# Attention heads two at a time, and expert weights with consecutive rows per partition, in a four-layer model on one core

## The chip, the core and the metric

The kernel runs on one core of a Trainium2 chip. The metric is the device time of one execution in microseconds (us). Three runs of the kernel before gave 1328.03 to 1331.99 us, median 1330.16.

Names in the profile: PE is TensorE (matmuls), PEld its weight loads, DVE is VectorE, ACT ScalarE, POOL GpSimd, SP the engine whose queue issues most DMAs. In a matmul, "64*128" is the part of the 128x128 array that it uses: rows (the contracted dimension) times columns. `out<-in` are the program's tile names.

## The reference

One sequence of 256 tokens (and 256 context tokens) of width 1024 goes through two blocks of two layers, all in f32. Cut to what matters here:

```
# block 1, two layers, latents and context: 8 query heads of 64, 2 key/value heads
p   = rms_norm(x) * (1 + scale) + shift  @ w_in
y_b = softmax(rope(q) k^T / 8) v            # 256 context + 256 latent keys
y_a = gmlp(...); y_c = bidirectional mLSTM(...)
x   = x + gate * concat(y_a, y_b, y_c) @ w_out
# block 2, layer 0: dilated attention, 3 groups of 16 heads, band of 128 keys + own block
logits = q k^T / 8 + rel_bias ;  the three groups merged by their softmax denominators
# block 2, layer 1: forgetting attention, 16 heads, causal
logits = q k^T / 8 + cum_t - cum_s ;  p = softmax(masked logits)
# after each of the two: mixture of 16 experts, the best group of 4, the best 2 in it
hid = silu(t @ w_gate[e]) * (t @ w_up[e])   # 1024 -> 256
y   = sum_e gate[e] * hid @ w_down[e]       # 256 -> 1024
x   = x + g_f * y
```

## The kernel before, in words

The 256 latents are two tiles of 128 tokens, the context another two (T is the tile). Most products are exact to f32 by splitting each factor into two f16 parts: `mm3` issues hi*hi, hi*lo and lo*hi, `mm3p` (L271) does the same for several products, one kind after the other in turns. Splitting costs an ACT copy and a VectorE subtraction per tile of weights (`wl<-raw,wh`, L418). All matmuls have the line of the helper `mm` (L258), transposes that of `tr` (L262), so tile names tell them apart.

The work around attention is woven: every head is a generator that yields an estimate of how long its next step should wait. `lane` keeps two of them active; `tick` and `step`, called between projection matmuls, advance the one whose time has come. After that a scheduler fixes, engine by engine, the order of instructions; from then on each engine runs its queue in order. PSUM has eight banks: two for projections (`ps_mm`), two for scores (`ps_s`), two for transposes (`ps_tr`), one for attention outputs (`ps_o`), one more (`ps_ad`).

- `attention` (block 1): `head(h)` issues three score matmuls with 64 contracted rows (512 or 256 keys) into one score bank, VectorE's maximum (L980) and ACT's exponential; after a yield the transposes of the probabilities, after another the products with the values.
- `attn2` (block 2, dilated and forgetting): the same with two query tiles per head, 128 and 256 keys. VectorE adds the bias and takes the extreme in one instruction (L1530). In the forgetting attention a matmul with all 128 rows (`ps_s<-nc,s`) first writes the bias into the bank.
- `head(h)` of even h lies in rows 0 to 63 of the array, that of odd h in rows 64 to 127.

The expert stages: `x_T` transposes the tokens for the router, `gather0` and `gather` pick the tokens of each expert by a product with one-hot matrices (`ps_s<-OH,nhl`, the token tile is the stationary operand), up to 64 tokens per expert. Experts go in eight pairs P: `gate_up(P)` (moving operand: the f32 weights), transposes of the hidden values (`ps_tr<-consts,mh`), `down` and `scatter` (`oh,OHT`). `moe_gu` issues the DMAs of gate and up weights from SP, 512 KB each for even P into the `raw` tiles, 256 KB each for odd P into tiles named `x`, two pairs ahead; `moe_dn` those of the down weights (`big`, `qk`). At P = 4 a branch on overflow stands in the program; all engines meet there, and the DMAs for P = 6 are issued behind it. In DRAM a row of w_gate or w_up is 256 f32 (1 KB), one of w_down 1024 f32 (4 KB).

Of the kernel before, what the change touches and what calls it, by code (L numbers as in the profile page):

```python
# [10 lines left out]
F32 = mybir.dt.float32  # L11
# [4 lines left out]
OP = mybir.AluOpType  # L16
# [46 lines left out]
def late_arrays(a):  # L63
# [11 lines left out]
    for l in range(2):  # L75
        c[f"rb_{l}"] = rep(np.concatenate([a["router_group_b_2"][l], a["router_expert_b_2"][l]]))
        wr = np.zeros((D, 32), np.float32)
        wr[:, :20] = np.concatenate([a["router_group_w_2"][l], a["router_expert_w_2"][l]], 1)
        c[f"wr_{l}"] = wr.reshape(8, 128, 32).transpose(1, 0, 2).reshape(128, 256)
# [29 lines left out]

def rep(v):  # L110
    return np.broadcast_to(np.asarray(v).reshape(1, -1), (128, v.size))
# [6 lines left out]
def param_arrays(a):  # L118
# [6 lines left out]
    for l in range(2):  # L125
        p[f"bada1_{l}"] = feat(a["b_ada"][l])
        p[f"bada2_{l}"] = feat(a["b_ada_2"][l])
        p[f"gn_{l}"] = feat(a["g_norm"][l])
        p[f"nm_{l}"] = feat(a["norm_mix_2"][l])
        p[f"nf_{l}"] = feat(a["norm_ffn_2"][l])  # L130
# [23 lines left out]
class Stage:  # L154
# [346 lines left out]
    def ada_feat(self, blk, l, v0, gname, res):  # L501
# [3 lines left out]
        def done(p):  # L505
            sb = self.w2("adasb")
            self.act(sb, p, AF.Copy)
            q = self.ps("tr")
            for b in range(4):
                self.tr(q[:, b * 128:(b + 1) * 128], sb[:, b * 128:(b + 1) * 128])  # L510
# [140 lines left out]
    def mod_T(self, xn, mods, xT, T):  # L651
# [3 lines left out]
        for k0 in (0, 4):  # L655
            p = self.ps("tr")
            for k in range(4):
                self.tr(p[:, k * 128:(k + 1) * 128], xn[:, (k0 + k) * 128:(k0 + k + 1) * 128])
# [70 lines left out]
class Block1(Stage):  # L729
# [233 lines left out]
    def attention(self, T, q, kTh, kTl, vh, vl, ybs):  # L963
# [6 lines left out]
        def head(h):  # L970
            a, j = h % 2, h // 2
            if h == 0:
                st["den"] = self.small("den", 8)
            den = st["den"]
            r = slice(64 * a, 64 * a + 64)
            h = 4 * a + j
            s = self.ps("s")
            self.mm3(s[:, :nk], qh[r, j], ql[r, j], kTh[r, :nk], kTl[r, :nk], True, True)
            mx = self.small("mx", 1, 4)
            nc.vector.tensor_reduce(mx, s[:, :nk], axis=AX.X, op=OP.max, negate=True)  # L980
            e = self.w2("e")
            self.act(e[:, :nk], s[:, :nk], AF.Exp, bias=mx, scale=1.0, accum_out=den[:, h:h + 1])
            yield 2.8
            et = self.ps("tr")
            for b in range(nb):
                self.tr(et[:, b * 128:(b + 1) * 128], e[:, b * 128:(b + 1) * 128])
            eh = self.h1("eh")
            el = self.h1("el")
            self.hilo(eh[:, :nk], el[:, :nk], et[:, :nk])
            yield 1.8  # L990
# [3 lines left out]
            for b in range(nb):  # L994
                Tk = (b + 2) % 4
                self.mm3(o[:, h * 64:h * 64 + 64], eh[:, b * 128:(b + 1) * 128],
                         el[:, b * 128:(b + 1) * 128], vh[:, Tk, r], vl[:, Tk, r], b == 0, b == nb - 1)
            if h == 7:
# [7 lines left out]
        return [head(h) for h in range(8)]  # L1006
# [342 lines left out]
class Block2(Block1):  # L1349
# [160 lines left out]
    def attn2(self, q, k, v, bias, nm, den, U, tail, extra=None):  # L1510
# [5 lines left out]
        def head(h):  # L1516
            b4, hh = divmod(h, 4)
            j, r = h // 2, slice(64 * (h % 2), 64 * (h % 2) + 64)
            s = self.ps("s")
# [7 lines left out]
            e = self.w2("e2")  # L1527
            bt = bias(h)
            for T, (c0, c1) in enumerate(spans):
                nc.vector.tensor_tensor_reduce(e[:, c0:c1], s[:, c0:c1], bt[:, 256 - (c1 - c0):256], op0=OP.add,  # L1530
                                               op1=OP.min, scale=-1.0, scalar=1e38, accum_out=nm[:, T, h:h + 1])
            for T, (c0, c1) in enumerate(spans):
                self.act(e[:, c0:c1], e[:, c0:c1], AF.Exp, scale=-1.0, bias=nm[:, T, h:h + 1],
                         accum_out=den[:, T, h:h + 1])
            yield 2.5
            et = self.ps("tr")
            for b in range(3):
                self.tr(et[:, b * 128:(b + 1) * 128], e[:, b * 128:(b + 1) * 128])
            eh = self.h1("e2h")
            el = self.h1("e2l")  # L1540
            self.hilo(eh[:, :384], el[:, :384], et[:, :384])
            yield 1.8
            if hh == 0:
                st["o"] = self.ps("o")
            o = st["o"]
            ov = o.rearrange("p (t h d) -> p t h d", t=2, h=4)
            vs = slice(h * 64, h * 64 + 64)
            for T, kb, b, first, last in ((0, 0, 0, True, True), (1, 0, 1, True, False), (1, 1, 2, False, True)):
                bb = slice(b * 128, b * 128 + 128)
                self.mm3(ov[:, T, hh], eh[:, bb], el[:, bb], v[0][:, kb, vs], v[1][:, kb, vs], first, last)  # L1550
            if hh == 3:
                self.act(U[:, :, b4 * 4:b4 * 4 + 4, :], ov, AF.Copy)
            if h == 7:
                yield from tail()

        return [head(h) for h in range(8)]
# [310 lines left out]

    def gather0(self, T):
# [3 lines left out]
        for k in range(8):  # L1872
            for a in range(2):
                self.mm(self.g0[k // 4][:, k % 4 * 128:k % 4 * 128 + 128], self.nhl[T][a][:, k * 128:k * 128 + 128],
                        self.OH[0][:, 256 * T:256 * T + 128], T == 0 and a == 0 and k % 4 == 0, T == 1 and a == 1 and k % 4 == 3)

    def moe_gu(self, i, P, part=range(8)):
# [3 lines left out]
        for q in part:  # L1881
# [3 lines left out]
            t = self.x4(F32, (2, 512)) if P % 2 else self.raw()  # L1885
# [3 lines left out]
            ws[a].extend(t[:, j] for j in range(n))  # L1889

    def moe_dn(self, i, P):
        ws = self.W2["dn", P] = []
        for a in range(2):
            t = (self.qk(F32, (8, 256)) if P % 2 else self.big()).rearrange("p (f n) d -> p f (n d)", f=2)
            self.nc.sync.dma_start(t, self.ap["w_down"][i, 2 * P + a].rearrange("(f p) n -> p f n", p=128))
            ws.append(t)

    def moe(self, i):
# [17 lines left out]
        def gather(c, half=None):  # L1916
# [3 lines left out]
            for k2 in range(4):  # L1920
                p = self.ps("s")
                for k in (2 * k2, 2 * k2 + 1):
                    o = p[:, n * (k % 2):n * (k % 2) + n]
                    dk = slice(k * 128, k * 128 + 128)
                    for m, (T, a) in enumerate(((0, 0), (1, 0), (0, 1), (1, 1))):
                        self.mm(o, self.nhl[T][a][:, dk], OH[c][:, 256 * T + h:256 * T + h + n], m == 0, m == 3)
# [64 lines left out]
        def gate_up(P):  # L1991
# [3 lines left out]
            for k in range(8):  # L1995
                for a in range(2):
                    xs = slice((2 * (P % 2) + a) * CAP, (2 * (P % 2) + a) * CAP + CAP)
                    self.mm(p[64 * a:64 * a + 64], x[k // 4][:, k % 4, xs], wg[a][k], k == 0, k == 7,
# [27 lines left out]
        for P in range(8):  # L2026
# [15 lines left out]
            q = self.ps("tr")  # L2042
            for f in range(2):
                self.tr(q[:, f * 128:(f + 1) * 128], h[:, f * 128:(f + 1) * 128])
# [23 lines left out]
    def overflow(self, i, cnt, CAP):  # L2068
# [3 lines left out]
        with tc.If(rv > CAP):  # L2072
# [7 lines left out]
            with tc.For_i(0, 16, 1) as e:  # L2080
                raws = []
                for q in range(4):
                    t = self.wtile(("wh", "wl")[q % 2], (2, 512), F32)
                    for n, nm in enumerate(("w_gate", "w_up")):
                        nc.sync.dma_start(t[:, :, n * 256:n * 256 + 256],
                                          ap[nm][i, ds(e, 1)].rearrange("a (k p) n -> p (a k) n", p=128)[:, 2 * q:2 * q + 2, :])
# [75 lines left out]
```

## Time and profile before

| | before |
|---|---|
| three runs, median (lowest, highest) | 1330.16 (1328.03, 1331.99) us |
| profiled execution: its time, its span | 1332.35, 1330.6 us |
| mean granted TensorE clock | 0.963 |
| PE busy | 1230.0 us (92%) |
| DVE, ACT, POOL busy | 775.6 (58%), 630.6 (47%), 226.3 us (17%) |
| DMA moved | 292.36 MB in 159870 packets, mean 220 GB/s |

The stages, in us of the span: block 1 to about 545 (first layer to 320), the dilated attention 545 to 850, its expert stage 885 to 1016, the forgetting attention 1024 to 1157, its expert stage 1190 to 1323. An engine's busy share is a mean over these. A granted clock of 1.00 is 2.4 GHz for TensorE. In a timeline row the figure after the start is the length from the first start to the last end of the instructions merged in the row; an idle time in brackets is the engine's before the row, with what ended it.

### The profile page before, as it was taken

Reading aid. Unit: us, or ns where it says so; the run is one execution under the profiler, and the core shown is the slowest. Engines: PE = TensorE matmul, PEld = TensorE weight load, DVE = VectorE, ACT = ScalarE, POOL = GpSimd, SP = SyncE. Lnnn points to the kernel's source line nnn. Section 1 sums busy time; section 2 is a strip of 40 time slices with the busy share of each in tenths; the row PEclk is TensorE's granted clock in tenths of the full one; section 3 lists DMA queues with packets and bytes.
Section 4 is the critical chain, followed back from the end, with each engine's and each line's share of the span. In section 5 each row is a group of like instructions: output and inputs, shape, how many; then the busy total and the mean of one; then the engine's idle time right before and its main releaser. Section 6 shows DMA issues by size and latency. Waiting matters only on the chain. (4 is left out here: it accounts for less than half of the span.)

```text
span 1330.6 us, 21270 instructions
## 1 busy us (share of the span) xinstructions
PE 1230.0 (92%) x8064; PEld 590.9 (44%) x8064; DVE 775.6 (58%) x1787; ACT 630.6 (47%) x1373; POOL 226.3 (17%) x254
## 2 busy tenths in 40 slices
PE   6889999999999998999999999989986999989987
PEld 2434444544444444445555555445322445545332
DVE  3585646785567768756777777562114676563212
ACT  3434545553545556566767776333114556432211
POOL 1021000221330001342224222010002412010000
PEclk8899999999999999999999999889998999779989
DMA  9744455344484474687454547779998785419995
GB/s 323 258 157 159 159 174 183 123 164 144 140 271 144 167 263 156 214 300 278 166 185 132 185 164 244 253 240 328 337 325 293 287 302 187 155 46 333 331 327 192
DMA packets 159870, 292.36 MB, mean 220 GB/s; under 512 B 10890, under 2 KB 94986, under 8 KB 153876
## 3 DMA queue, kind: packets, MB, share of 16 engines
q1 hardware_dynamic: 157028, 281.57, 61.8%
q0 software_dynamic: 2736, 9.39, 2.3%
q8 instruction: 65, 1.06, 0.3%
q14 instruction: 41, 0.34, 0.1%
HBM read 288.80 MB, written 2.13 MB: 219 GB/s over the span
## 5 line engine op out<-in xcount | busy, mean ns | idle before, releaser
L258 PE MATMUL ps_mm<-wh,x 128*128 128x512 f16 (+1 forms) x1120 | 379.1, 379 | 3.6 <-DVE kn L245 1.8
L258 PEld LDWEIGHTS <-x 128*128 128x128 f16 (+1 forms) x2344 | 194.0, 98 | 250.5 <-issue 80.6
L258 PE MATMUL ps_mm<-wl,x 128*128 128x512 f16 (+1 forms) x736 | 276.8, 376 | 0.0
L418 DVE SCALAR_TENSOR_TENSOR wl<-raw,wh 128x1024 f16<-128x1024 f32 (+2 forms) x188 | 221.6, 1209 | 52.7 <-ACT wh L242 52.2
L242 ACT ACTIVATE wh<-raw 128x1024 f16<-128x1024 f32 (+2 forms) x188 | 182.2, 1015 | 47.1 <-PE ps_mm L258 40.7
L258 PE MATMUL ps_mm<-wh,y 128*128 128x512 f16 (+1 forms) x480 | 175.3, 379 | 0.0
L258 PE MATMUL ps_ad<-raw,cz 128*32 128x512 f32 (+1 forms) x640 | 113.4, 578 | 12.8 <-DMA raw<-in_w_ada 12.8
L287 POOL TENSOR_SCALAR hss<-hss 128x8 f32<-128x8 f32 (+2 forms) x58 | 18.5, 319 | 430.2 <-DVE hss L683 415.0
L288 POOL TENSOR_TENSOR hr<-hss,nhalf 128x8 f32<-128x8 f32 (+2 forms) x58 | 85.0, 1466 | 4.8
L258 PEld LDWEIGHTS <-y 128*128 128x128 f16 x560 | 55.3, 101 | 63.3 <-issue 13.0
L253 DVE SCALAR_TENSOR_TENSOR oh<-ps_tr,ka,oh 128x512 f16<-128x512 f32 x32 | 24.0, 751 | 91.5 <-ACT oh L242 88.7
L242 ACT ACTIVATE e<-e,ka 128x128 f32<-128x128 f32 (+1 forms) x128 | 56.7, 445 | 42.9 <-DVE ka L1530 41.7
L262 PE MATMUL ps_tr<-consts,e 128*128 128x128 f32 x352 | 57.7, 285 | 6.0 <-ACT e L242 3.0
L258 PE MATMUL ps_mm<-wh,big 128*128 128x512 f16 x192 | 59.5, 386 | 0.5 <-DVE big L253 0.5
L262 PEld LDWEIGHTS ps_tr<-consts,e 128*128 128x128 f32 x352 | 42.2, 144 | 28.4 <-ACT e L242 8.8
L242 ACT ACTIVATE oh<-ps_tr,ka 128x512 f16<-128x512 f32 x32 | 22.0, 687 | 58.0 <-PE ps_tr L258 58.0
L258 PE MATMUL ps_mm<-raw,wh 128*64 128x512 f32 x128 | 37.7, 665 | 8.0 <-DMA raw<-in_w_up 8.0
L245 DVE TENSOR_TENSOR el<-ps_tr,eh 128x512 f16<-128x512 f32 (+1 forms) x48 | 27.8, 597 | 29.3 <-ACT eh L242 29.0
L245 DVE TENSOR_TENSOR e2l<-ps_tr,e2h 128x384 f16<-128x384 f32 x64 | 34.8, 554 | 16.7 <-ACT e2h L242 16.4
L242 ACT ACTIVATE e2h<-ps_tr 128x384 f16<-128x384 f32 x64 | 30.4, 486 | 28.7 <-PE ps_tr L262 28.4
L242 ACT ACTIVATE e<-ps_s,mx 128x512 f32<-128x512 f32 (+1 forms) x48 | 29.3, 613 | 30.9 <-DVE mx L980 28.2
L258 PEld LDWEIGHTS ps_ad<-raw,cz 128*32 128x32 f32 x640 | 21.3, 112 | 50.5 <-issue 35.7
(377 smaller groups left out, 2005.0 us busy)
## 6 DMA issues: line engine op xcount, KB each, us to landing
raw<-in_w_ada SPq DMA_DIRECT2D x40, 1024.0 KB
raw<-in_a_w_in SPq DMA_DIRECT2D x36, 1024.0 KB
raw<-in_w_ada SPq DMA_DIRECT2D x64, 512.0 KB
raw<-in_w_in SPq DMA_DIRECT2D x16, 1024.0 KB
qk<-in_w_down SPq DMA_DIRECT2D x16, 1024.0 KB
big<-in_w_down SPq DMA_DIRECT2D x16, 1024.0 KB
x<-in_w_gate SPq DMA_DIRECT2D x64, 256.0 KB
raw<-in_w_gate SPq DMA_DIRECT2D x32, 512.0 KB
```

The costliest lines, as they stand in the source:

```text
L242: return self.nc.scalar.activation(out, in_, func, **kw)
L245: return self.nc.vector.tensor_tensor(out, a, b, op=op)
L253: return self.nc.vector.scalar_tensor_tensor(out, a, s, b, op0=op0, op1=op1)
L258: return self.nc.tensor.matmul(out, lhsT, rhs, start=start, stop=stop, **kw)
L262: return self.nc.tensor.transpose(out, in_, self.C("ident")[:n, :n])
L287: self.nc.gpsimd.tensor_scalar(in_, in_, eps, None, op0=OP.add)
L288: self.nc.gpsimd.tensor_tensor(out, in_, self.nhalf.to_broadcast(list(in_.shape)), op=OP.pow)
L418: (on or self.nc.vector).scalar_tensor_tensor(wl, raw, WS, wh, op0=OP.mult, op1=OP.subtract)
```

## The change

Two parts.

First, the order in which the 1024 features lie over partitions and tiles in the expert stages. The DMAs of w_gate and w_up give each partition four consecutive rows (4 KB in one piece for even P, and two of the four, 2 KB, for odd P) in place of single rows of 1 KB; those of w_down two consecutive rows (8 KB). So feature 4p + j of each half of 512 belongs to partition p, and all that meets the weights follows: the gather reads its stationary operand in steps of four f16 (`rows`), the transposes of the router (`x_T`), of the modulation (`nf`), and of the hidden values (`hv`) read f32 in steps of four or two, and constants are laid out anew on the host (`quad`).

Second, `head(h)` becomes `pair(j)`: both heads' score matmuls go in turns into the two score banks, then come both softmaxes, the transposes of one head (a yield of 1.0) and of the other (1.8), the values of one (0.3) and of the other. `mm3p` ties each matmul to the one before, so that the scheduler keeps them in turns. A lane now runs over four pairs in place of eight heads.

```diff
     def mm3p(self, parts, start=True, stop=True):
+        last = None
         for m in range(3):
             for o, ah, al, bh, bl in parts:
-                self.mm(o, al if m == 2 else ah, bl if m == 1 else bh, start and m == 0, stop and m == 2)
+                i = self.mm(o, al if m == 2 else ah, bl if m == 1 else bh, start and m == 0, stop and m == 2).ins
+                if last is not None:
+                    self.tc.add_manual_dep(i, last.name, mybir.DependencyInfo(
+                        mybir.DependencyClass.NoSync, mybir.DependencyReason.DATA), reason="in turns")
+                last = i
...
-            s = self.ps("s")
-            self.mm3(s[:, :nk], qh[r, j], ql[r, j], kTh[r, :nk], kTl[r, :nk], True, True)
+            s = [self.ps("s") for _ in range(2)]
+            self.mm3p([(p[:, :nk], qh[r, j], ql[r, j], kTh[r, :nk], kTl[r, :nk]) for p, r in zip(s, self.rows2)])
+            es = []
+            for a in range(2):
+                mx = self.small("mx", 1, 4)
+                nc.vector.tensor_reduce(mx, s[a][:, :nk], axis=AX.X, op=OP.max, negate=True)
...
                 if extra is not None:
-                    self.mm(s[:, c0:c1], extra[0][:, h:h + 1].to_broadcast([128, 128]), extra[1][:, :n], True, False)
+                    for p, h in zip(s, hs):
+                        self.mm(p[:, c0:c1], extra[0][:, h:h + 1].to_broadcast([128, 128]), extra[1][:, :n], True, False)
                 tq = slice(T * 128, T * 128 + 128)
-                self.mm3(s[:, c0:c1], q[0][r, j, tq], q[1][r, j, tq], k[0][r, j, :n], k[1][r, j, :n],
-                         extra is None, True)
+                self.mm3p([(p[:, c0:c1], q[0][r, j, tq], q[1][r, j, tq], k[0][r, j, :n], k[1][r, j, :n])
+                           for p, r in zip(s, self.rows2)], extra is None, True)
...
-        return [head(h) for h in range(8)]
+        return [pair(j) for j in range(4)]
...
+        xv = self.x[T][:, 512 * n:512 * n + 512].rearrange("p (n k) -> p k n", k=4)
         for k in range(4):
-            self.tr(p[:, k * 128:(k + 1) * 128], self.x[T][:, (4 * n + k) * 128:(4 * n + k + 1) * 128])
+            self.tr(p[:, k * 128:(k + 1) * 128], xv[:, k])
...
+    def rows(self, T, a, k):
+        h = self.nhl[T][a][:, k // 4 * 512:k // 4 * 512 + 512]
+        return h.rearrange("p (n j) -> p j n", j=4)[:, k % 4]
...
-                src = self.ap[nm][i, 2 * P + a].rearrange("(k p) n -> p k n", p=128)
-                self.nc.sync.dma_start(t[:, :, m * 256:m * 256 + 256], src[:, k:k + n, :])
+                src = self.ap[nm][i, 2 * P + a].rearrange("(h p j) n -> p h j n", h=2, j=4)
+                self.nc.sync.dma_start(t[:, m], src[:, k // 4, k % 4:k % 4 + n, :])
...
-            self.nc.sync.dma_start(t, self.ap["w_down"][i, 2 * P + a].rearrange("(f p) n -> p f n", p=128))
+            self.nc.sync.dma_start(t, self.ap["w_down"][i, 2 * P + a].rearrange("(p f) n -> p f n", p=128))
```

What this moves on TensorE, at two places. The first is the first pair of heads in the forgetting attention: `ps_s_11458` is the bank of one head, `ps_s_11472` (before) or `ps_s_11459` (now) that of the other, `nc3_10991` the moving operand of the bias matmul, `qk_10994` the queries and keys. Before, from the bias matmul of the first head's 256 keys on:

```order
L258 LDWEIGHTS s3_10992
L258 MATMUL ps_s_11458<-nc3_10991,s3_10992 128x256
L258 LDWEIGHTS qk_10994
L258 MATMUL ps_s_11458<-qk_10994 128x256
L258 LDWEIGHTS qk_10994
L258 MATMUL ps_s_11458<-qk_10994 128x256
L258 LDWEIGHTS qk_10994
L258 MATMUL ps_s_11458<-qk_10994 128x256
L258 LDWEIGHTS s3_10992
L258 MATMUL ps_s_11472<-nc3_10991,s3_10992 128x128
L258 LDWEIGHTS qk_10994
```

Now, from the start of the pair on:

```order
L264 LDWEIGHTS s3_10992
L264 MATMUL ps_s_11458<-nc3_10991,s3_10992 128x128
L264 LDWEIGHTS s3_10992
L264 MATMUL ps_s_11459<-nc3_10991,s3_10992 128x128
L264 LDWEIGHTS qk_10994
L264 MATMUL ps_s_11458<-qk_10994 128x128
L264 LDWEIGHTS qk_10994
L264 MATMUL ps_s_11459<-qk_10994 128x128
L264 LDWEIGHTS qk_10994
L264 MATMUL ps_s_11458<-qk_10994 128x128
L264 LDWEIGHTS qk_10994
```

Before, a bias matmul stands ahead of each run of three 64-row matmuls of one head. Now the two heads' bias matmuls stand together, and six 64-row matmuls follow them, one of each head in turns.

The second place is in the dilated attention, on TensorE again. Before, where the first head of a pair ends and the second begins (banks `ps_s_6708` and `ps_s_6720`):

```order
L258 MATMUL ps_s_6708<-qk_6266 128x256
L258 LDWEIGHTS qk_6266
L258 MATMUL ps_s_6708<-qk_6266 128x256
L258 LDWEIGHTS qk_6266
L258 MATMUL ps_s_6720<-qk_6266 128x128
L258 LDWEIGHTS qk_6266
L258 MATMUL ps_s_6720<-qk_6266 128x128
L258 LDWEIGHTS qk_6266
L258 MATMUL ps_s_6720<-qk_6266 128x128
L258 LDWEIGHTS qk_6266
```

Now, at the second of two pairs that follow each other (banks `ps_s_6804` and `ps_s_6805`; the first pair's twelve score matmuls stand 6 matmuls ahead, in turns without a break); `ps_mm` rows are projections:

```order
L264 MATMUL ps_mm_6722<-wl_6562,x2_6012 128x512
L264 LDWEIGHTS qk_6266
L264 MATMUL ps_s_6804<-qk_6266 128x128
L264 LDWEIGHTS x2_6012
L264 MATMUL ps_mm_6722<-wh_6561,x2_6012 128x512
L264 LDWEIGHTS x2_6012
L264 MATMUL ps_mm_6722<-wh_6561,x2_6012 128x512
L264 LDWEIGHTS x2_6012
L264 MATMUL ps_mm_6722<-wl_6562,x2_6012 128x512
L264 LDWEIGHTS qk_6266
L264 MATMUL ps_s_6805<-qk_6266 128x128
L264 LDWEIGHTS qk_6266
```

The second pair's first matmul stands apart from the other eleven, with three projections between. The first pair of every two is whole, in the forgetting attention too; in the order of the whole program about half of all pairs have such a break. Between two such pairs and the next two there are 73 to 171 other matmuls in the dilated attention, where before every pair stood some 51 (between units 102 to 110) from the next.

## Rows read from the trace of the kernel before

**Rows 1.** Windows by stretch (busy us and count by engine, granted clock, DMA share, GB/s).

```profile
core 0: us, PE busy (x) PEld busy (x) DVE busy (x) ACT busy (x) POOL busy (x), PEclk, DMA share, GB/s
70.00:180.00 110.00, 106.37 (x774) 48.12 (x772) 67.50 (x168) 46.67 (x104) 12.80 (x12) 0.97 0.44 145
590.00:850.00 260.00, 250.90 (x1841) 133.04 (x1840) 186.88 (x412) 174.20 (x394) 71.73 (x69) 1.00 0.60 205
885.00:1016.00 131.00, 123.93 (x630) 48.89 (x628) 34.68 (x98) 29.79 (x65) 1.17 (x2) 0.97 0.94 317
1076.00:1157.00 81.00, 80.43 (x564) 43.69 (x562) 51.99 (x123) 47.95 (x115) 13.32 (x14) 0.95 0.61 207
1190.00:1323.00 133.00, 125.05 (x624) 50.08 (x624) 34.37 (x98) 28.42 (x61) 1.16 (x2) 0.96 0.85 289
```

**Rows 2.** Timeline of TensorE around one lone head, first layer (start, us, line, operation, count).

```profile
107.75 0.38 PE L258 MATMUL ps_mm<-wl,x 128*128 128x512 f16 x1
107.96 0.38 PE L258 MATMUL ps_mm<-wh,y 128*128 128x512 f16 x1
108.27 0.82 PE L258 MATMUL ps_s<-x,x 64*128 64x512 f16 x3
109.02 0.44 PE L262 MATMUL ps_tr<-consts,qo 128*128 128x128 f32 x2
```

**Rows 3.** Timeline of TensorE, two heads next to each other, second layer.

```profile
431.78 0.83 PE L258 MATMUL ps_s<-x,x 64*128 64x512 f16 x6
```

**Rows 4.** Timeline of TensorE, two heads of the forgetting attention.

```profile
1076.66 0.22 PE L258 MATMUL ps_s<-nc,s 128*128 128x128 bf16 x1
...
1078.81 0.39 PE L258 MATMUL ps_mm<-wh,x 128*128 128x512 f16 x1
```

**Rows 5.** Timeline of TensorE, two heads of the dilated attention.

```profile
618.71 0.80 PE L258 MATMUL ps_s<-qk 64*128 64x128 f16 x12
619.43 0.39 PE L258 MATMUL ps_mm<-wh,x 128*128 128x512 f16 x1
```

**Rows 6.** Timeline of VectorE after two dilated heads.

```profile
599.52 0.29 DVE L1530 CUSTOM_DVE_ANT_0 e<-ps_s,big 128x128 f32<-128x128 f32 x1
...
599.73 0.42 DVE L1530 CUSTOM_DVE_ANT_0 e<-ps_s,big 128x256 f32<-128x256 f32 x1
...
600.08 1.22 DVE L418 SCALAR_TENSOR_TENSOR wl<-raw,wh 128x1024 f16<-128x1024 f32 x1
```

**Rows 7.** Longest wait of TensorE in each expert stage (total, times, longest).

```profile
PE ps_mm L258 <- DMA raw<-in_w_up: 3.6, 1, 3.6
...
PE ps_mm L258 <- DMA raw<-in_w_up: 4.4, 1, 4.4
```

**Rows 8.** Chain that ended last, second expert stage.

```profile
1274.03 8.61 DMA raw<-in_w_up
```

**Rows 9.** Windows: gate and up rows alone; down rows among them; after the second wait.

```profile
955.00:961.00 6.00, 6.00 (x29) 2.11 (x28) 1.49 (x2) 1.38 (x2) 0.00 (x0) 1.00 1.11 349
985.00:990.00 5.00, 5.00 (x26) 1.62 (x24) 0.21 (x1) 0.00 (x0) 0.00 (x0) 1.00 1.04 403
1280.00:1300.00 20.00, 17.23 (x61) 5.35 (x62) 1.64 (x4) 2.14 (x4) 0.00 (x0) 0.83 1.08 366
```

**Rows 10.** Timeline of TensorE before and after that wait: two scatter matmuls each.

```profile
1271.32 0.59 PE L258 MATMUL ps_o<-oh,OHT 128*128 128x512 f16 x2
...
1285.76 1.06 PE L258 MATMUL ps_o<-oh,OHT 128*128 128x512 f16 x2
```

**Rows 11.** Timeline of TensorE, a gather of 16 matmuls.

```profile
894.55 1.07 PE L258 MATMUL ps_s<-OH,nhl 128*128 128x128 f16 x16
895.45 0.55 PE L258 MATMUL ps_tr<-kb,OH 128*128 128x6 f16 x16
```

**Rows 12.** Weight loads by form (busy, mean ns, idle before).

```profile
L262 PEld LDWEIGHTS ps_tr<-consts,e 128*128 128x128 f32 x352 | 42.2, 144 | 28.4 <-ACT e L242 8.8 <-DVE qk L253 4.4 <-ACT e2h L242 0.8
...
L258 PEld LDWEIGHTS <-nhl 128*128 128x128 f16 x320 | 28.8, 108 | 12.0 <-issue 9.4
```

More of the change, by code (lines that the diff above doesn't have):

```diff
@@ L107, in feat, with quad @@
     return np.ascontiguousarray(v.reshape(-1, 128).T)
+def quad(v):
+    return np.ascontiguousarray(v.reshape(-1, 128, 4).transpose(1, 0, 2).reshape(128, -1))
 def rep(v):
@@ L968, in attention, with pair @@
         st = {}
[L970 to L972 removed]
+        def pair(j):
+            if j == 0:
                 st["den"] = self.small("den", 8)
             den = st["den"]
[L975 to L990 removed]
+            s = [self.ps("s") for _ in range(2)]
[4 more added lines that the diff above has]
+                nc.vector.tensor_reduce(mx, s[a][:, :nk], axis=AX.X, op=OP.max, negate=True)
+                e = self.w2("e")
+                self.act(e[:, :nk], s[a][:, :nk], AF.Exp, bias=mx, scale=1.0, accum_out=den[:, 4 * a + j:4 * a + j + 1])
+                es.append(e)
+            yield 2.8
+            eT = []
+            for a in range(2):
+                et = self.ps("tr")
+                for b in range(nb):
+                    self.tr(et[:, b * 128:(b + 1) * 128], es[a][:, b * 128:(b + 1) * 128])
+                eh = self.h1("eh")
+                el = self.h1("el")
+                self.hilo(eh[:, :nk], el[:, :nk], et[:, :nk])
+                eT.append((eh, el))
+                yield (1.0, 1.8)[a]
             if "o" not in st:
@@ L993, in head @@
             o = st["o"]
[L994 to L998, printed above, removed]
+            for a, r in enumerate(self.rows2):
+                h = 4 * a + j
+                eh, el = eT[a]
+                for b in range(nb):
+                    Tk = (b + 2) % 4
+                    self.mm3(o[:, h * 64:h * 64 + 64], eh[:, b * 128:(b + 1) * 128],
+                             el[:, b * 128:(b + 1) * 128], vh[:, Tk, r], vl[:, Tk, r], b == 0, b == nb - 1)
+                if not a:
+                    yield 0.3
+            if j == 3:
                 rec = self.small("rec", 8)
@@ L1514, in attn2, with pair @@
         st = {}
[L1516 to L1519, printed above, removed]
+        def pair(j):
+            hs = (2 * j, 2 * j + 1)
+            s = [self.ps("s") for _ in hs]
             for T, (c0, c1) in enumerate(spans):
@@ L1527, in head @@
[L1527 to L1534, printed above, removed]
@@ new lines, in pair @@
+            es = []
+            for p, h in zip(s, hs):
+                e = self.w2("e2")
+                bt = bias(h)
+                for T, (c0, c1) in enumerate(spans):
+                    nc.vector.tensor_tensor_reduce(e[:, c0:c1], p[:, c0:c1], bt[:, 256 - (c1 - c0):256], op0=OP.add,
+                                                   op1=OP.min, scale=-1.0, scalar=1e38, accum_out=nm[:, T, h:h + 1])
+                for T, (c0, c1) in enumerate(spans):
+                    self.act(e[:, c0:c1], e[:, c0:c1], AF.Exp, scale=-1.0, bias=nm[:, T, h:h + 1],
+                             accum_out=den[:, T, h:h + 1])
+                es.append(e)
@@ new lines, in pair @@
+            yield 2.5
+            eT = []
+            for a in range(2):
+                et = self.ps("tr")
+                for b in range(3):
+                    self.tr(et[:, b * 128:(b + 1) * 128], es[a][:, b * 128:(b + 1) * 128])
+                eh = self.h1("e2h")
+                el = self.h1("e2l")
+                self.hilo(eh[:, :384], el[:, :384], et[:, :384])
+                eT.append((eh, el))
+                yield (1.0, 1.8)[a]
+            for a, h in enumerate(hs):
+                b4, hh = divmod(h, 4)
+                if hh == 0:
+                    st["o"] = self.ps("o")
+                o = st["o"]
+                eh, el = eT[a]
+                ov = o.rearrange("p (t h d) -> p t h d", t=2, h=4)
+                vs = slice(h * 64, h * 64 + 64)
+                for T, kb, b, first, last in ((0, 0, 0, True, True), (1, 0, 1, True, False), (1, 1, 2, False, True)):
+                    bb = slice(b * 128, b * 128 + 128)
+                    self.mm3(ov[:, T, hh], eh[:, bb], el[:, bb], v[0][:, kb, vs], v[1][:, kb, vs], first, last)
+                if hh == 3:
+                    self.act(U[:, :, b4 * 4:b4 * 4 + 4, :], ov, AF.Copy)
+                if not a:
+                    yield 0.3
+                elif j == 3:
+                    yield from tail()
@@ L1558, in dilated @@
+        return [pair(j) for j in range(4)]
     def dilated(self, xT):
```

52 lines of the change are left out of this document (19 added, 33 removed).

## The prediction

> **What bounds the kernel now.** I read the windows first. In the five stretches that the change touches, TensorE is busy 106.4 of 110 us, 250.9 of 260, 123.9 of 131, 80.4 of 81 and 125.1 of 133 us [rows 1], while VectorE stays under three quarters. So time comes off where matmuls go, and is added wherever TensorE has to wait. Next I read the waits of the two expert stages: one wait each for expert weights, 3.6 and 4.4 us [rows 7], and the chain that ended last begins at the second one [rows 8]. The timeline then gives the price of the score matmuls themselves.
>
> **Scores: the prices.** A lone head with 512 keys is three matmuls over 64 rows. It starts at 108.27 and the next matmul at 109.02: 0.75 us, though three steps of 0.213 (107.75 to 107.96 is one step of ordinary 512-column matmuls, 0.21) would be 0.64; and the matmul ahead of it started 0.31 earlier instead of 0.21 [rows 2]. So each crossing between 64-row and 128-row work costs about 0.10 us. Where two heads stand next to each other, as three of one and then three of the other, six matmuls are listed with 0.83 us from the first start to the last end [rows 3], where one head's three have 0.82 [rows 2]: as long as one head alone, so 0.76 to the next start. The chip already runs both array halves together when the heads are merely adjacent; what matters is adjacency and the number of crossings, not the alternation.
>
> **Scores: the sum by stage.** (a) First layer, first two tiles (70 to 180 us): 16 heads, before nearly all alone or three matmuls apart, at 0.75 + 0.10. That is 13.6 us. Now 8 pairs at 0.76 + 0.10 = 6.9, but in the new order five of them are broken: the first head's first matmul stands alone and the other five follow some projections later (the second excerpt shows the pattern in the dilated attention). A break is two more crossings plus a lone matmul's half that no longer overlaps, 0.20 + 0.11 = 0.3; seven breaks add 2.1. Gain 13.6 - 9.0 = 4.6, taken as 4.5. (b) Forgetting attention, 8 pairs. Before, each head's bias matmul (all 128 rows) stands between the 64-row runs: 1076.66 to 1078.81 is 2.15 us a pair [rows 4], four 64-row runs with eight crossings. Serially the columns are 4 x (128 + 256) x 2 = 3072 at 0.213 us for 512, 1.28 us; the other 0.87 is eight crossings. Now there are two runs a pair: two bias matmuls of each width 0.32, the 64-row matmuls at half of 0.96 = 0.48, four crossings 0.44, sum 1.24. Gain 0.9 for the four whole pairs and 0.63 for the four broken ones: 6.1. If the halves did not overlap here, 0.48 more a pair, and the gain would be 2.3. (c) Dilated attention, 24 pairs. These already stood adjacent: twelve matmuls from 618.71 to 619.43, 0.72 us [rows 5]. Alternated they need at least 0.48 + 0.10, so a whole pair gains 0 to 0.14 (I take 0.07 for 12 of them, 0.8), while the other 12, the second of every two, are broken and lose 0.2 to 0.25 (2.7); against that, five breaks of before go (1.0). Loss about 1. Second layer of block 1 and the 256-key tiles: adjacent before, one or two more breaks now, 0.1 loss. Sum of (a) to (c): 4.5 + 6.1 - 1.1 = 9.5 us off TensorE, with 5 to 13 as bounds.
>
> **Scores: the new wait.** Two lanes now carry pairs, so one pair follows the last after some 6 to 12 projections, and both score banks must be free again. TensorE takes instructions in order, so all projections of the next lane queue behind a score matmul that waits. A dilated head leaves its bank after two VectorE instructions of 0.29 and 0.42 us (0.21 + 0.35 apart), and a weight split of 1.22 us can stand between [rows 6]. Pair 0 runs 0.65 us, six to eight fillers 1.3 to 1.7; two heads on VectorE are 1.3 us. Without a split ahead the banks are free in time; with one, TensorE waits up to 1.2 us. There are 28 such second pairs (12 in block 1, 12 dilated, 4 forgetting), so the bounds are 0 and 34 us. I take 3, one wait of 0.3 in three: VectorE has 28% slack in that stretch [rows 1], and the order puts a split between two pairs only after the first pair's reductions.
>
> **Expert weights.** The gate and up rows grow from 1 KB to 4 KB (even pairs of experts) and 2 KB (odd), the down rows from 4 to 8 KB. In a stretch where only 1 KB rows were under way the DMA gave 349 GB/s at a share of 1.11; where 4 KB rows of the down weights were among them 403 at 1.04 [rows 9]. Taking that ratio, 0.87, the transfer that TensorE waits for, 8.61 us [rows 8], shortens by 1.15 in each stage: 2.3 in all. It cannot vanish, because its issue stands behind the branch on overflow, a barrier that the change leaves. Behind the second wait two scatter matmuls take 1.06 us, and 0.59 ahead of it [rows 10]; the granted clock of the 20 us from 1280 on is 0.83 [rows 9], a part of them at the lower of its two levels, 1.2 instead of 2.4 GHz. The eight scatter matmuls pay 4 x 0.47 = 1.9 us. A shorter idle stretch may spare part; I take 1.0. Late chunks elsewhere give 0.5. Sum 3.8, bounds 0 (rows are not faster) and 15 (all idle time of both stages, 7.1 + 7.9 by [rows 1]).
> The Trainium skill's "DMA: Bandwidth & Descriptors" (Specifications) names 512 B as the size from which transfers run at line rate, and about 358 GB/s as what the HBM gives one core. By that nothing here is gained and the forecast would be 3.8 later. The 403 in [rows 9] is above that figure, so the trace does not bear it out.
>
> **Strided operands.** To match, the gather reads its stationary operand in steps of 8 bytes (320 loads), and 72 transposes read f32 in steps of 16 or 8 bytes. No row shows a strided load. From below: nothing changes, since gather matmuls of 128 columns start every 0.056 us (16 from 894.55 to 895.45 [rows 11]) while a load is listed with 98 to 108 ns [rows 12], so loads overlap. From above: the loads double and nothing hides it, 320 x 0.1 = 32 us, and 72 transposes x 2 records x 0.14 [rows 12] = 20 us more. I take 0, the nearest row being the overlap.
> By the Trainium skill's "SBUF — State Buffer" (Specifications, and the cacheline note in "SBUF: two separate sides") two accesses must fall in one 16-byte line for full speed. That clears the f16 gather and speaks against the transposes with 16-byte steps. No run here shows it. If those 40 transposes doubled, it would be up to 11 us by [rows 12].
>
> **Sum.** Own time of the profiled execution 1332.35 (span 1330.6 and 1.75 around it). 1332.35 - 9.5 + 3 - 3.8 = 1322.0. The three runs have a median of 1330.16, 2.2 below that execution: 1320.
>
> **Rivals.**
> 1. The pairs wait on their banks (slower). One mechanism: a split or another VectorE job stands ahead of the reductions of the pair before. Gains are 13.3, so the point where it turns slower by 4 is 17.3 / 28 = 0.62 us a pair, half a split. With a whole split each time: 1330 - 13 + 34 = 1351; with 0.75 us, 1338. For: the score lanes move in bursts now, four heads' exponentials and evacuations at once. Against: VectorE's slack, and almost no TensorE wait in [rows 1] for the dilated stretch. Chance 0.11.
> 2. TensorE gets shorter but stages end elsewhere. Block 1's tiles and the forgetting stage end in chains of VectorE and GpSimd; if (a) and (b) are given back there, only the expert part stays: 1330 - 3.8 + 1 = 1327. For: the first layer's two tiles leave 3.6 of 110 us idle, so not every step there waits for TensorE. Against: 80.4 of 81 us busy [rows 1]. Chance 0.18.
> 3. The expert stages are transfer-bound, and faster rows also take the clock dip and both waits: 8.0 + 2 x 1.9 = 11.8 instead of 3.8: 1312. For: DMA share 0.94 in the first stage [rows 1]. Against: TensorE is fully busy between the waits. Chance 0.15.
> 4. Strided loads cost half of their upper bound for the gather, +16: 1336. Chance 0.07.
> The forecast itself, 1313 to 1326, has 0.49.
>
> **The numbers.** A measurement of this kernel tells 0.3% (4 us) from no change. Faster: the forecast, rival 3 and a quarter of rival 2, 0.69. Same: most of rival 2, and the mild ends of 1 and 4, 0.18. Slower: the rest of rivals 1 and 4, 0.13. Range 1307 to 1336: it takes in rivals 2, 3 and 4 and leaves out most of rival 1.
>
> **What would show it.** In the forgetting stage a pair's 16 matmuls should span about 1.25 us instead of 2.15, or 1.45 broken; in the first layer six matmuls 0.76. The waits of scores on VectorE's reductions should sum to a few us; over 15 would be rival 1. The expert waits should be near 2.5 and 3.3 us, the DMA above 390 GB/s with even pairs. The gather's 16 matmuls should still take 0.90 us; above 1.5 is rival 4. I am wrong if the forgetting window does not shrink, or if the dilated stretch grows by more than 3 us.

## The result, and the profile after

The changed kernel takes 1312.0 us in the median of four executions (1307.47 to 1317.39), where the kernel before has 1331.08 beside it: ratio 0.9855, 95% interval 0.9807 to 0.9903. Two later sets, on two different chips, gave 0.9842 (0.9819 to 0.9865) and 0.9851 (0.9823 to 0.9879). The forecast was 1320 us with a range of 1307 to 1336: the right way, inside the range, and half the size. Executions of one program differ here by 4 to 18 us, mostly along with the granted clock that they get (six of the pairs-only kernel below: 1315.59 us at 0.975 to 1322.69 at 0.967), so single stages are compared over several profiles further on. The profiled execution of the changed kernel took 1307.47 us (span 1305.5, clock 0.979), its fastest.

The windows that answer to the dilated and the forgetting attention of [rows 1], moved by what had been gained until then (us, then busy us and count of PE, PEld, DVE, ACT, POOL, then granted clock, DMA share, GB/s):

```profile
591.00:844.00 253.00, 247.27 (x1827) 126.85 (x1829) 185.25 (x419) 174.24 (x398) 79.38 (x68) 1.00 0.59 202
1065.00:1137.00 72.00, 70.09 (x545) 37.52 (x543) 50.52 (x122) 46.10 (x114) 14.82 (x14) 1.00 0.68 247
```

TensorE is about as full as it was: 247 of 253 us and 70 of 72. In the forgetting attention the granted clock is 1.00 instead of 0.95. The lengths of these windows are not yet the gain, because they do not hold quite the same work (1827 matmuls of TensorE where [rows 1] had 1841, and 545 where it had 564); the stages are measured between the same instructions in the table further on.

**Score matmuls after.** First layer, TensorE's timeline: a whole pair and a broken one, answering to [rows 2, 3].

```profile
143.95 0.82 PE L264 MATMUL ps_s<-x,x 64*128 64x512 f16 x6
144.71 0.39 PE L264 MATMUL ps_mm<-wh,x 128*128 128x512 f16 x1
...
146.37 0.37 PE L264 MATMUL ps_s<-x,x 64*128 64x512 f16 x1
...
148.94 0.82 PE L264 MATMUL ps_s<-x,x 64*128 64x512 f16 x5
149.69 0.39 PE L264 MATMUL ps_mm<-wh,x 128*128 128x512 f16 x1
```

Six matmuls take 0.76 us, where a lone head's three took 0.75. In a broken pair the first matmul stands 2.6 us ahead of the other five, and those five still take 0.75.

Forgetting attention: first the 64-row matmuls of one head before, which stand inside [rows 4], then a whole pair now and the start of a broken one.

```profile
1076.81 0.34 PE L258 MATMUL ps_s<-qk 64*128 64x128 f16 x3
...
1077.30 0.50 PE L258 MATMUL ps_s<-qk 64*128 64x256 f16 x3
```

```profile
1065.49 0.28 PE L264 MATMUL ps_s<-nc,s 128*128 128x128 bf16 x2
1065.69 0.34 PE L264 MATMUL ps_s<-qk 64*128 64x128 f16 x6
1065.97 0.39 PE L264 MATMUL ps_s<-nc,s 128*128 128x256 bf16 x2
1066.29 0.50 PE L264 MATMUL ps_s<-qk 64*128 64x256 f16 x6
1066.72 0.39 PE L264 MATMUL ps_mm<-wh,x 128*128 128x512 f16 x1
...
1068.45 0.22 PE L264 MATMUL ps_s<-nc,s 128*128 128x128 bf16 x1
1068.60 0.23 PE L264 MATMUL ps_s<-qk 64*128 64x128 f16 x1
```

From 1065.49 to 1066.72 is 1.23 us; before it was 2.15, and the forecast was 1.24. Six 64-row matmuls are listed with 0.34 and 0.50 us, as long as three were.

Dilated attention, answering to [rows 5]: a whole pair, then the next one, broken, which waited 0.53 us for VectorE.

```profile
608.93 0.67 PE L264 MATMUL ps_s<-qk 64*128 64x128 f16 x12
609.53 1.07 PE L264 MATMUL ps_ad<-raw,cz 128*32 128x512 f32 x8
...
611.66 0.21 PE L264 MATMUL ps_s<-qk 64*128 64x128 f16 x1 [0.53 <-DVE ka L1556]
...
612.56 0.67 PE L264 MATMUL ps_s<-qk 64*128 64x128 f16 x11
```

A whole pair now takes 0.60 instead of 0.72 us. The waits of TensorE in the dilated stage (total us, times, longest), before from 598 to 865:

```profile
PE ps_o L258 <- DVE e2l L245: 3.7, 8, 1.3
PE ps_tr L262 <- DVE x L245: 3.2, 2, 1.7
PE ps_tr L262 <- DVE qk L253: 2.3, 9, 0.4
```

and after, from 594 to 861:

```profile
PE ps_s L264 <- DVE ka L1556: 3.8, 5, 0.8
PE ps_tr L268 <- DVE x L251: 0.9, 1, 0.9
PE ps_tr L268 <- DVE qk L259: 0.4, 2, 0.2
PE ps_o L264 <- DVE e2l L251: 0.3, 1, 0.3
```

The new wait is there with 3.8 us. What the forecast lacks is the other side: 9.2 us of waits of before became 1.6. (Before there is one wait more, 1.1 us for the weights `in_w_ada`. It is also missing with the weights alone, without pairs, so it is not counted here.)

**Expert stages after.** Their waits, first and second stage, answering to [rows 7]; the piece of the chain that answers to [rows 8]; two windows to [rows 9] and a scatter behind the second wait to [rows 10]:

```profile
PE ps_mm L264 <- DMA raw<-in_w_up: 2.0, 1, 2.0
...
PE ps_mm L264 <- DMA raw<-in_w_up: 2.2, 1, 2.2
```

```profile
1251.68 6.97 DMA raw<-in_w_up
```

```profile
964.00:970.00 6.00, 3.99 (x12) 1.54 (x11) 0.75 (x1) 1.07 (x2) 0.00 (x0) 0.74 1.02 408
970.00:976.00 6.00, 6.00 (x29) 2.00 (x29) 0.75 (x1) 0.69 (x1) 0.00 (x0) 0.97 1.03 421
```

```profile
1260.42 0.59 PE L264 MATMUL ps_o<-oh,OHT 128*128 128x512 f16 x2
```

The transfer takes 6.97 us instead of 8.61 (0.81 of it), the DMA moves 408 to 421 GB/s instead of 349, the waits are about half. No single wait is fixed: in four profiles with 1 KB rows the two waits add up to 8.0 to 8.9 us, in six with longer rows to 2.2 to 5.9. Behind the second one two scatter matmuls take 0.59 us as ahead of it, not 1.06; in the first stage the clock still dips, to 0.74 in the window of the wait.

### The profile page after: what moved, and what is told of

The parts are those of the page before. It is cut to its first block, busy times and chain, and to the rows that moved or that the text cites. A ratio compares the mean times of both kernels' runs of the same rounds, so it can differ in the third digit from the quotient of the medians.

```text
span 1305.5 us, 21252 instructions
## 1 busy us (share of the span) xinstructions
PE 1207.0 (92%) x8064; PEld 574.9 (44%) x8064; DVE 771.4 (59%) x1787; ACT 628.1 (48%) x1373; POOL 237.3 (18%) x254
## 3 DMA queue, kind: packets, MB, share of 16 engines
q8 instruction: 65, 1.06, 0.3%
## 5 line engine op out<-in xcount | busy, mean ns | idle before, releaser
L264 PEld LDWEIGHTS <-x 128*128 128x128 f16 (+1 forms) x2344 | 189.2, 98 | 245.9 <-issue 91.0
L299 POOL TENSOR_TENSOR hr<-hss,nhalf 128x8 f32<-128x8 f32 (+2 forms) x58 | 90.5, 1561 | 4.8
L264 PEld LDWEIGHTS <-big 128*128 128x128 f16 x288 | 28.1, 98 | 32.4 <-DVE big L259 0.3
```

Source lines behind the costliest of these rows:

```text
L264: return self.nc.tensor.matmul(out, lhsT, rhs, start=start, stop=stop, **kw)
L299: self.nc.gpsimd.tensor_tensor(out, in_, self.nhalf.to_broadcast(list(in_.shape)), op=OP.pow)
```

## The experiments

Each ratio is against runs of the kernel before on the same chip, with its 95% interval. The stage lengths are distances between first instructions in the profiles: first layer (first score matmul to last `ps_tr<-consts,yb`), second layer (on to the first `consts,qn`), dilated (first `qk` score to the first `ps_tr<-x,szb`), forgetting (first `nc` to the next first `x,szb`), both expert stages (first `raw,wh` to the last scatter of the first stage, and to the end for the second). A profile counts to the column whose attention order, or whose weight layout, it has; the kernels with whole pairs, further down, are left out, and so is the attention of the one that goes head after head.

| stage, us | heads one at a time, or 1 KB rows | pairs, or longer rows | difference of means | forecast |
|---|---|---|---|---|
| first layer | 235.6 234.1 236.2 236.3 234.2 | 231.9 233.6 231.7 233.1 231.7 | -2.9 | -4.5 |
| second layer | 254.6 258.1 257.8 255.6 258.3 | 257.2 258.4 257.5 256.7 254.4 | -0.1 | +0.1 |
| dilated | 271.9 271.7 270.2 271.4 | 266.4 266.3 266.8 266.4 266.4 266.4 | -4.8 | +1, and the new wait +3 |
| forgetting, to the second router | 97.6 95.4 96.1 | 87.7 87.8 87.8 87.7 87.9 88.2 87.9 | -8.5 | -6.1 |
| both expert stages | 271.1 271.6 274.6 273.7 | 268.9 269.0 265.2 268.2 267.6 267.8 266.9 | -5.1 | -3.8 |

The differences sum to -21.4 us; the three timings of the changed kernel say -19 to -21.

### The weights alone

```diff
-    (pair(j), mm3p tied)          # of the changed kernel
+    (head(h), mm3p as before)
```

> The weights part alone: attention heads one at a time, as in the kernel before. Theory A (the pairs carry the gain: fewer crossings and overlapped halves): the two expert waits shrink to about 2 us each, as in the changed kernel (2.0 and 2.2), so 3 to 5 us come off: 1326 to 1328, ratio 0.996 to 0.998. Theory B (longer rows carry it, also by a steadier clock in the expert stages and behind them): 10 us or more, below 1321. If strided operands cost something of size: no gain or slower than before.

Measured: 1323.09 us, ratio 0.9974 (0.9949 to 0.9999). In that profile the two expert waits are 4.0 and 0.5 us, not the 2 us each that were expected, though their sum is as expected. Theory A holds: the longer rows bring 0.3%, not the bulk. That strided operands cost nothing of size is bounded too: the gain is about what the shorter transfers give.

### The pairs alone, twice

```diff
-    (weights in rows of four, rows(), quad(), strided transposes)   # of the changed kernel
+    (weights, gather and transposes as before)
```

> The pairs alone, with the expert weights and all operands as before. Theory A: 14 to 16 us come off, 1315 to 1317, ratio about 0.988; the forgetting pair's 16 matmuls take 1.24 us and the expert waits stay near 3.6 and 4.4. Theory B: 5 to 9 us, 1322 or later.

Measured: 1320.02 us, ratio 0.9941 (0.992 to 0.9962), less than theory A asked for and inside what theory B did. The stages spoke against it: forgetting 87.8 and dilated 266.4, as short as with the weights. So it was run again:

> The pairs alone once more. By the stage sums of ten profiles (forgetting -8.5, dilated -4.8, first layer -3.1, second +0.2) it should be 14 to 16 us under before, ratio 0.988 to 0.9895; the first timing said 0.9941. If that holds again, weights and pairs help each other by some 9 us in a way that the stages don't show; if it comes to 0.989, its first timing was three executions at a lower clock.

Measured: 1318.02 us, ratio 0.9895 (0.9873 to 0.9918), that is 14 us. With the weights' 0.9974 this makes 0.987, where the changed kernel on the same chip had 0.9851: the parts add up within their intervals, as theory A has it. The interval of the first set does not meet that of the second. Three of its six executions lay at 1315.6 to 1318.2 with clocks of 0.973 to 0.975, three at 1321.8 to 1322.7 with 0.966 to 0.969, but that is the smaller part: the medians of the pairs-only kernel differ by only 2.0 us (1320.02 and 1318.02), those of the kernel before beside it by 5.3 (1327.68 on the first chip, 1332.98 on the second). So by timing alone the pairs are worth 8 to 15 us; that it is the upper end rests on the stages, which are alike in both profiles.

### Turns, or only next to each other

```diff
-        for m in range(3):
-            for o, ah, al, bh, bl in parts:
+        for o, ah, al, bh, bl in parts:      # mm3s, used for the scores; still tied
+            for m in range(3):
```

> The changed kernel with each pair's score matmuls tied in the order of three of one head and then three of the other, in place of turns. Adjacency theory (the halves overlap whenever heads are next to each other): six 512-column matmuls stay at 0.76 us, twelve dilated ones go from 0.60 back to 0.72, the forgetting pair from 1.24 to about 1.3; 24 x 0.12 + 1 = 4 us at most over the changed kernel, 1312 to 1316. Rival (only turns overlap the halves): 0.96 for a dilated pair and 1.7 for a forgetting one, 24 x 0.36 + 8 x 0.5 + 8 x 0.5 = 17 us over it, 1325 or later.

Measured: 1320.4 us, ratio 0.9936 (0.9915 to 0.9957), later than adjacency expected and earlier than the rival. TensorE's timeline tells why. Dilated attention, a whole pair and the first head of a broken one:

```profile
619.65 0.68 PE L264 MATMUL ps_s<-qk 64*128 64x128 f16 x12
620.26 1.07 PE L264 MATMUL ps_ad<-raw,cz 128*32 128x512 f32 x8
...
622.38 0.65 PE L264 MATMUL ps_s<-qk 64*128 64x128 f16 x6 [0.52 <-DVE ka L1567]
622.97 0.39 PE L264 MATMUL ps_mm<-wh,x 128*128 128x512 f16 x1
```

A whole pair takes 0.61 us, as in turns and not the 0.72 that was expected, so turns are not what overlaps the halves. But in this order a break falls between the two heads, three and three, and then nothing overlaps: one head alone takes 0.59 us, as long as a whole pair. In block 1 twelve runs of three 512-column matmuls stand alone in this order, where the changed kernel has one. The first and second layer became 235.9 and 262.2 us in this profile, 3.5 and 5.4 over the means of pairs in turns; in the second a granted clock of 0.98 instead of 0.99 to 1.00 has a part that is not told apart. So the turns most likely matter by keeping a broken pair cheap: one matmul alone, five together.

### The kernel before, and the changed kernel, again

> The kernel before once more, with a second profile: what two executions of one program differ by. Ratio 0.997 to 1.003. If the stretches at a lower granted clock (0.93 in 823 to 870, 0.94 in the forgetting stage, 0.72 in the second router) belong to the program, they come back at the same places; if they are chance, they lie elsewhere and the stage sums differ by 2 to 4 us.

> The changed kernel once more, as the yardstick on this chip. If weights and pairs simply add up (0.9974 x 0.9941): ratio 0.9915, 11 us. If the first measurement of 0.9855 was typical and the parts help each other: 0.984 to 0.987, 17 to 21 us.

> The changed kernel as the yardstick on this chip: ratio 0.983 to 0.986.

Measured: before against itself 1.0002 (0.998 to 1.0023); the changed kernel 0.9842 (0.9819 to 0.9865) and 0.9851 (0.9823 to 0.9879). The second profile of before has the forgetting stage at 95.4 us with a granted clock of 0.96, the first 97.6 with 0.91, and in seven profiles with pairs it lies at 0.96 to 0.98. A lower clock in part of that stage thus comes back in the order of before, though not fixed in size, and the two ranges meet at 0.96. It is clearer in the last 47.5 us ahead of the first router: granted clock 0.93 and 0.96 in the two profiles of before, 0.96 in the two others with single heads in the dilated attention (weights alone, pairs in the forgetting attention alone), 1.00 in all six with dilated pairs in turns:

```profile
823.40:870.90 47.50, 45.65 (x325) 19.68 (x324) 27.60 (x77) 19.69 (x57) 3.63 (x3) 0.96 0.78 268
```

```profile
815.90:863.40 47.50, 46.27 (x349) 21.23 (x348) 30.49 (x80) 21.74 (x60) 3.24 (x3) 1.00 0.75 258
```

The first is the second profile of before, the second that of the changed kernel's second set. Why the clock falls there in the one order only, no run here shows.

### Pairs stage by stage

Block 1 as before, pairs in block 2:

```diff
-        return [pair(j) for j in range(4)]     # attention() of block 1
+        return [head(h) for h in range(8)]
```

> The changed kernel with block 1's attention one head at a time as before; pairs only in the dilated and the forgetting attention. Stage theory: the first layer's 4 us come back and nothing else: 0.3% over the changed kernel, about 0.988 to 0.990 of before. Rival (block 1's gain is eaten by its second layer, 254.6 to 257.8 in the profiles): the same as the changed kernel within 2 us.

Pairs in the forgetting attention alone:

```diff
+        if extra is None:                      # dilated: heads one at a time
+            return self.attn2h(q, k, v, bias, nm, den, U, tail)
```

> The changed kernel with pairs in the forgetting attention alone. Stage theory: 7 to 10 us of the pairs' gain and the weights' 3 to 4 stay: ratio 0.990 to 0.992, and 4 to 5 us less gain than with dilated pairs (whole pairs 0.60 instead of 0.72 us, fewer waits). Rival: the dilated pairs bring nothing (breaks against overlap, my forecast was a loss of 1 us): the same as the run with pairs in both.

Measured: 0.99 (0.9866 to 0.9934) and 0.9925 (0.99 to 0.995), on one chip with the changed kernel's 0.9842. So weights and forgetting pairs give 10.6 of the 20.1 us by the medians; the dilated pairs come next (the intervals of these two overlap, but the stage is 266.8 us in one and 271.4 in the other, so the rival for them is out); block 1's pairs take the rest, more than the 3 us that its stages show. The first of the two spread from 1308.45 to 1326.02 us, with clocks from 0.977 to 0.963; how block 1's share divides into work and clock stays open.

### Whole pairs

```diff
+    def both(self, i, free):
+        if free is not None:       # free: the last reader of the other score bank
+            self.tc.add_manual_dep(i, free.name, mybir.DependencyInfo(
+                mybir.DependencyClass.Sync, mybir.DependencyReason.DATA), reason="both banks")
...
+                if last is None:
+                    self.both(i, free)
```

> The changed kernel, but a pair's first score matmul also waits for the last reader of the other score bank, so that no pair is broken (the order then has 6 or 12 in turns nearly everywhere). If a break costs its two crossings and a lone matmul, 0.145 + 0.1 + 0.1 in the dilated attention and 0.4 in the first layer, some 24 breaks are worth 6 us: about 1306. Rival: the time moves into the wait, since TensorE now waits for both banks at once: 1310 to 1316, with waits of scores on VectorE of 8 us or more in the dilated stage in place of 3.8.

> Whole pairs everywhere, beside the changed kernel on one chip: 2 to 5 us under it (its median was 1306.75 on a chip where before had 1327.68). If the waits for both banks eat it: within 1 us of it.

> Whole pairs (the first score matmul waits for both banks) in the dilated and the forgetting attention alone, block 1 as in the changed kernel. Stage sums of the profiles: dilated 266.4 to 264.7 and forgetting 88 to 85.5, block 1 unchanged: 4 us under the changed kernel, and 0 to 3 us under whole pairs everywhere if the longer second layer of that profile (261.8 instead of 257) belongs to its order; the same as it if that was chance of the clock.

Measured: whole pairs everywhere 0.9833 (0.9809 to 0.9856) and 0.981 (0.9784 to 0.9835); in block 2 alone 0.9853 (0.9826 to 0.988); the changed kernel beside the last two 0.9851. So whole pairs everywhere are 5 us under it in one set (1307.7 against 1313.0 us), with intervals that just overlap. From the profile of the second run, the second of two dilated pairs, which in the changed kernel is the broken one, and the wait:

```profile
615.97 0.67 PE L264 MATMUL ps_s<-qk 64*128 64x128 f16 x12 [0.44 <-DVE ka L1567]
```

```profile
PE ps_s L264 <- DVE ka L1567: 3.3, 5, 0.7
```

The wait does not grow (3.3 us for 3.8), and the stages are 264.7 (dilated) and 85.5 us (forgetting), 1.7 and 2.4 less. The rival, that the time moves into the wait, is out. Whole pairs in block 2 alone have 264.6 and 87.2 us, but their timing shows no gain over the changed kernel; its six executions run from 1303.68 to 1318.56. That whole pairs everywhere beat the changed kernel is likely, not settled.

## Why the prediction was right, and where it was short

- **The price of a pair: right.** A whole forgetting pair was put at 1.24 us and takes 1.23; six 512-column matmuls at 0.76 and take 0.76; dilated between 0.58 and 0.72 and is 0.60. That adjacency and not alternation makes the overlap was right, as the head-after-head order shows.
- **(a), first layer, 4.5 us: 2.9.** The matmuls went as said, but part of the gain was given back in waits. The stage before, then after, and TensorE's longest waits in each:

```profile
83.80:319.40 235.60, 225.18 (x1698) 107.79 (x1699) 152.44 (x354) 115.38 (x270) 26.67 (x38) 0.99 0.46 155
80.70:312.50 231.80, 218.62 (x1700) 104.58 (x1700) 152.28 (x354) 114.35 (x270) 28.20 (x38) 1.00 0.47 158
```

```profile
PE ps_tr L262 <- POOL yc L690: 3.8, 3, 1.5
PE ps_tr L262 <- ACT e L242: 2.5, 1, 2.5
```

```profile
PE ps_tr L268 <- POOL yc L704: 5.0, 3, 2.1
PE ps_s L264 <- ACT e L248: 2.8, 2, 2.5
PE ps_s L264 <- ACT vnh L248: 2.0, 2, 1.0
```

Busy time fell by 6.6 us, idle time grew from 10.4 to 13.2. The scores' wait for ACT's exponentials (2.8 us) stands in the place of one of the transposes for the same tiles (2.5), so it adds almost nothing. What came in are waits of other work of the layer, on `vnh` and on GpSimd's `yc`: rival 2 in a small measure.
- **(b), forgetting, 6.1 us: 8.5.** A whole pair went as said. To keep the clock apart from the work, here is the stage at one granted clock, in the second profile of before, then in that of pairs in block 2:

```profile
1077.50:1172.90 95.40, 91.97 (x629) 49.35 (x627) 59.29 (x134) 52.76 (x125) 14.98 (x16) 0.96 0.58 196
1066.60:1154.30 87.70, 84.36 (x630) 45.80 (x628) 58.51 (x134) 51.42 (x125) 16.53 (x16) 0.96 0.60 213
```

At 0.96 in both the stage is 7.7 us shorter, with 7.6 us less of busy time. So the lower clock of the other two profiles with single heads (0.91 and 0.93) is the smaller part of the 8.5. What the work gives beyond 6.1 probably comes from the last two pairs of before: their eight 64-row runs stood in twelve pieces, between 1145.5 and 1153.6 us of the trace of before, where the forecast took 2.15 us for all eight pairs. No run prices this by itself.
- **(c), dilated, a loss of 1 us and most of the new wait: 4.8 us gained.** This is the step that failed. The stretch up to the merge of the last group, before and after:

```profile
598.70:823.10 224.40, 215.33 (x1571) 117.83 (x1571) 165.91 (x355) 159.19 (x352) 70.01 (x67) 1.00 0.57 191
```

```profile
594.60:816.30 221.70, 216.25 (x1572) 113.48 (x1572) 163.55 (x355) 159.38 (x352) 78.34 (x67) 1.00 0.57 193
```

Busy time even grew by 0.9, as the breaks let one expect, at the same clock. It is idle time that fell, from 9.1 to 5.5 us, which leaves 2.7 us. The other 2.8 of the 5.5 between these two profiles lie in the last stretch ahead of the router, 2.3 of them in busy time at a granted clock of 1.00 instead of 0.93. The forecast added the new wait, but it counted no wait that goes: the products with the values no longer stand so close behind VectorE's `e2l` (3.7 us to 0.3), nor the transposes behind `qk` (2.3 to 0.4) and `x` (3.2 to 0.9). These are the idle us of the dilated window in [rows 1] that the forecast called almost no wait. It is the dilated pairs that take them away: with pairs in the forgetting attention alone the three waits are still 3.7, 2.3 and 3.2 us.
- **The new wait, 3 us: 3.8 in the dilated stage, 2.8 in the first layer, 0.4 in the forgetting attention.** The place was right, the size is over twice the 3 us, far from the 15 that would have been rival 1. In the dilated stage it did no harm, because more waits went than came.
- **Expert weights, 3.8 us: 5.1 over all profiles.** Transfers are faster and the waits shorter, as said; with the weights alone the timing has 3.5 us by the ratio. The ratio of transfer time was 0.81 rather than 0.87, perhaps because [rows 9] held only some of the longer rows. That the wait could not vanish was wrong: behind the branch, in the second stage, it is 0 to 2.5 us over six profiles with longer rows (none in the changed kernel's second set).
By the Trainium skill's "DMA: Bandwidth & Descriptors" (Specifications), rows from 512 B up run at line rate and HBM gives one core some 358 GB/s. The trace does not agree: 349 GB/s with 1 KB rows, 408 to 421 with 2 to 8 KB.
- **Strided operands, 0: right as far as the timing tells.** A gather of 16 matmuls takes 0.92 us, where [rows 11] had 0.90:

```profile
886.32 1.08 PE L264 MATMUL ps_s<-OH,nhl 128*128 128x128 f16 x16
887.24 0.55 PE L2025 MATMUL ps_tr<-kb,OH 128*128 128x128 f16 x7
```

- **Rivals 2 to 4** did not come, but for the 2 to 3 us of rival 2 in the first layer. The measured 1312.0 us lies 1 us under the forecast's own 1313 to 1326 and is the very figure of rival 3. Rival 3 is not its cause: it asked for 11.8 us from the expert stages, which gave 5.1, and the rest came from attention. The gather did not slow.

Summed up: the direction came from the right mechanism in the forgetting attention, the first layer and the expert stages. The size was half, mainly because the dilated stage's old waits were left out; to a smaller part because of the lower clock that the order of before had at the end of that stage and in the forgetting one, and of the latter's broken pairs. By the table these two stages give 13.3 us where the forecast, with the new wait, had 2.

## What to carry to other kernels

In this kernel matmuls that use one half of the array overlap with those of the other half when they are neighbours in the queue (twelve take 0.60 us in turns, 0.61 head after head), and each change between 64-row and full-height work costs about 0.1 us, so count crossings in the order, not instructions. When a reordering adds a wait, list the waits that it takes away with the same care: both come from the same queues. Where two tiles must be free before a group can run whole, letting its first instruction wait for both is worth a try: here it shortened the two stages by 1.7 and 2.4 us, while the gain of the whole is likely and not settled.

## What the runs showed of the hardware

Longer rows also made SP's own issue faster. SP's queue at P = 6 of the second expert stage, the same DMA before and after (start, us, DMA):

```profile
1278.08 3.02 SPq L1888 DMA_DIRECT2D raw<-in_w_up  x1
```

```profile
1253.63 0.45 SPq L1930 DMA_DIRECT2D raw<-in_w_up  x1
```

This is the sixth of eight DMAs of 512 KB that are issued one behind the other. Over the eight an issue takes 0.4 to 3.0 us with rows of 1 KB and 0.3 to 0.6 us with rows of 4 KB. It goes with the rows and not with the pairs: the pairs alone have issues of up to 2.5 us there, the weights alone 0.8 at most.

An f32 transpose whose input is read in steps has a longer weight load. The loads of the hidden values, before and with steps of 8 bytes (ns min/median/max):

```profile
L262 PEld LDWEIGHTS ps_tr<-consts,mh x32: 138/141/183, 911.3 to 1316.5; 128*128 128x128 f32 x32
```

```profile
L268 PEld LDWEIGHTS ps_tr<-consts,mh x32: 194/196/220, 900.4 to 1289.7; 128*128 128x128 f32 x32
```

That is 55 ns more each, some 4 us over the 72 strided transposes if all of it showed. By the Trainium skill's "SBUF — State Buffer" (Specifications) two accesses to one 16-byte line run at full speed; with 8-byte steps there are two, and the load is longer all the same.
